# A two-layer attention trunk on one core: first heads' stage length, place of the rotary tables, engine of the accumulators' first step, and order of the output projection

## The chip, the core and the metric

The kernel runs on one core of one Trainium2 chip. The metric is the device time of one execution in microseconds (us). The core's engines work side by side, each through its own queue in order: TensorE (PE: matrix products, with PEld for the loading of the stationary operand), VectorE (DVE), ScalarE (ACT), GpSimd (POOL) and SyncE (SP), which issues most of the DMAs here. They wait for each other on semaphores.

## What is computed

One sequence of 256 positions and 2048 features in float32 passes through two layers. Layer 0 mixes positions by a forgetting attention ("FoX", 16 heads of 128), layer 1 by sliding-window attention; each is followed by a gated feed-forward network with a short convolution. Every sub-layer is modulated by vectors that come from a conditioning vector c:

```python
c_act = jax.nn.silu(c)
for i in range(DEPTH):
    mod = c_act @ ada_w[i] + ada_b[i]
    sh1, sc1, g1, sh2, sc2, g2 = jnp.split(mod[:, None, :], 6, axis=-1)
    h = x * (1.0 + sc1) + sh1
    y = fox_attention(h, ...) if i % 2 == 0 else swa_attention(h, positions, ...)
    x = layer_norm(DEEPNORM_ALPHA * x + (1.0 + g1) * y, ln_mix_g[i], ln_mix_b[i])
    h = x * (1.0 + sc2) + sh2
    y = conv_ffn(h, ...)
    x = layer_norm(DEEPNORM_ALPHA * x + (1.0 + g2) * y, ln_ffn_g[i], ln_ffn_b[i])
```

In FoX a forget gate adds a cumulated bias to the scores:

```python
s = jnp.einsum('bqhd,bkhd->bhqk', qb, kb) * scale + cqb[..., None] - cum[:, :, None, :]
p = jax.nn.softmax(jnp.where(causal, s, -jnp.inf), axis=-1)
o = jnp.einsum('bhqk,bkhd->bqhd', p, v)
return o @ w_o
```

The rotary tables (sine and cosine of the positions) are used in layer 1 alone.

## The kernel before

**Weights.** Every weight matrix streams through in tiles of 256 rows by 512 columns (`stream`). SyncE loads a tile `w` into one of ten buffers, ScalarE casts it to the rounded format of the products (`wh`, L276), VectorE subtracts to get the residual (`wl`, L287), and PE multiplies by both parts, by `wh` first. Each tile is one step of the program; behind it the step calls `run_post` (results that were waiting to be taken over from PSUM), `feed` and `tick`. Casts and residuals each have four buffers, which PE frees. I number the tiles from 0. FoX uses 0 to 127: 0 to 44 in the opening (all of block 0's projections and parts of the other three), 45 to 56 for block 1, 57 to 74 for block 2, 75 to 95 for block 3, and 96 to 127 in the output projection, where two tiles hold four of the sixteen heads for one of four blocks of output columns.

**Heads.** A block makes q, k and v of four heads (0 to 3 in block 0, and so on). `head` and `attend` are generators, which `later(gens, lag)` puts on a list; one of them is started with each tile, and each goes one stage further every `lag` tiles: scores on PE (tile `S`), mask, maximum and softmax (tile `pr`: VectorE L693, exponentials on ScalarE L697, reciprocal on VectorE L703, scaling on ScalarE L705), transposition on PE (`T`, L717) with a copy on ScalarE (`pT`), and the product with v (`o`), which is split into a high and a low half (`oT`, or `hHL` for the last four heads). The heads of a block run beside the tiles of the next. `evac_v` starts them with a lag of 2.

**Background work.** The same list holds `columns` (bias and convolution columns), `rotary` (two DMAs on GpSimd's queue, a cast of the positions, a transposition on PE, some twenty small VectorE instructions, two sines on ScalarE) and `scaled`, which multiplies x by a constant on ScalarE. They are put on it ahead of block 0's step, in the line `later([forget(), columns(), rotary(), scaled()])`.

**Modulation vectors.** The ten vectors of `ada_list` are made beside all this by `ada_vector`: 32 loads `wa` for each, and 32 VectorE instructions of 128x1024 into the single tile `acc`. The first for each half is a product (L404), the others multiply and add (L406); then PE sums over partitions. `ada_tick` spends a rate for each tile, one load and one instruction for each whole unit. After the vector (0, 4) the making is held until the next sub-layer begins, so FoX makes exactly three: (0, 2), (0, 3) and (0, 4).

**Order.** Most instructions may be moved by a scheduler at build time; those under `pin(..., True)` stay in program order on their engine. So the order in which the instructions stand was read from the two built programs.

**Output projection.** `out_proj` takes output blocks 0 and 1 through heads 0 to 7 and 8 to 11, then, as the last heads become ready, through 12 to 15, and then blocks 2 and 3 whole. `residual` takes each block over on VectorE (L621, L622, L624). Behind it `modulate` normalises x (ScalarE L644, VectorE L646), keeps PE awake with idle products (`warm`), and builds the input of the feed-forward network ("the ramp").

Of the kernel before, what the change touches and what calls it, by code (L numbers as in the profile page):

```python
# [21 lines left out]
KC = D // P  # L22
# [19 lines left out]
def hybrid_trunk(ctx: ExitStack, tc: tile.TileContext, a: dict, out: bass.AP):  # L42
    nc = tc.nc
# [28 lines left out]
    def x_banks():  # L72
        return [bank("xs") for _ in range(NT)]
# [136 lines left out]
    def then(fn):  # L210

        work.append(fn)
        if len(work) == 1 and not ahead[0]:
            settle()
# [32 lines left out]
    def defer(gen):  # L247

        post.append(gen)
# [111 lines left out]
    def later(gens, lag=1):  # L361

        bg["wait"].extend((g, lag) for g in gens)
# [23 lines left out]
    cols = {}  # L387
    gates = {}
    ada_list = [(0, 2), (0, 3), (0, 4), (0, 5), (1, 0), (1, 1), (1, 3), (1, 2), (1, 4), (1, 5)]
    ada = {"gen": None, "debt": 0.0, "rate": 0.0, "gate_free": True}  # L390

    def ada_vector(l, v):
        row = v % 3 == 2
        acc = cst.tile([P, D], F32, tag="acc", name="acc")
        part = lambda c, n: acc[:, c:c + n]
        step_ = D // 2
        for k in range(KC):
            for c in range(0, D, D // 2):
                w = wtile("wa").rearrange("p a f -> p (a f)")
                pin(nc.sync.dma_start(w, a["ada_w"][l, k * P:(k + 1) * P, v * D + c:v * D + c + D // 2]), False)  # L400
                for o in range(0, D // 2, step_):
                    ac, wo = part(c + o, step_), w[:, o:o + step_]
                    if k == 0:
                        pin(nc.vector.tensor_scalar_mul(ac, wo, cact[:, 0:1]), True)  # L404
                    else:
                        pin(nc.vector.scalar_tensor_tensor(ac, wo, cact[:, k:k + 1], ac,  # L406
                                                           op0=ALU.mult, op1=ALU.add), True)
                yield
        if row:
            while not ada["gate_free"]:  # L410
                yield
            ada["gate_free"] = False
            g = cst.tile([P, D], F32, tag="gate", name="gate")
            nc.gpsimd.dma_start(g, a["ada_b"][l, v * D:(v + 1) * D].partition_broadcast(P))
            for j in range(D // 512):
                ps = bank()
                mm(ps, ones, acc[:, j * 512:(j + 1) * 512], start=True, stop=True)
                yield
                gj = g[:, j * 512:(j + 1) * 512]
                nc.vector.scalar_tensor_tensor(gj, ps, 1.0, gj, op0=ALU.add, op1=ALU.add)  # L420
            gates[l, v] = g
            return
        ps = bank()
        for k in range(KC):
            pin(mm(ps[:, k:k + 1], part(k * P, P), ones[:, 0:1], start=True, stop=True))
            if k % 4 == 3:
                yield
        cv = cst.tile([P, KC], F32, tag=f"cv{v}", name="cv")
        pin(nc.vector.scalar_tensor_tensor(cv, ps[:, :KC], 1.0 if v % 3 else 0.0,
                                           acol[:, l, v * KC:(v + 1) * KC], op0=ALU.add, op1=ALU.add), True)  # L430
        cols[l, v] = cv
        if v == 4:
            ada["held"] = True
# [15 lines left out]
    def ada_need(l, v):  # L449
        n = 0  # L450
        while (l, v) not in cols and (l, v) not in gates:
            ada_step()
            n += 1
        if n:
            print("caught up", l, v, n)
# [278 lines left out]
    def out_proj(oT, full, w_o, l):  # L734
        def stat(kc, t):
            while kc not in full:
                step()
            return oT[kc][0][:, t * P:(t + 1) * P], oT[kc][1][:, t * P:(t + 1) * P]

        ps = {d: x_banks() for d in range(2)}  # L740

        def part(d, ks):
            use = x_mm_end(ps[d], stat, KC, 2) if d == D // WB - 1 else                 lambda kc, h, l_: x_mm(ps[d], kc, h, l_, stat, KC - 1)
            stream(w_o, 0, d * WB, ks, use)

        for i, ks in enumerate((range(0, 8), range(8, 12))):
            then(lambda i=i: ada.update(rate=((1.4,1.4,1.8,1.8), (0.9,)*4)[l][i]))
            for d in range(2):
                part(d, list(ks))
        then(lambda: ada_need(l, 2))  # L750
        for d in range(D // WB):
            if d < 2:
                part(d, list(range(12, KC)))
            else:
                then(lambda d=d: ada.update(rate=((1.4,1.4,1.8,1.8), (0.9,)*4)[l][d]))
                ps[d] = x_banks()
                part(d, list(range(KC)))
            then(lambda d=d: defer(residual(ps[d], d, gates[l, 2], True)))
        then(lambda: (flush(), ada.update(gate_free=True)))


    def fox(l, j):
# [57 lines left out]
        ready = []  # L820
        oT, full = {}, set()

        def evac_v(ps, V, then, old):
            ps = ps()
            for t in range(NT):
                if old:
                    v = old[t]
                    nc.vector.tensor_tensor(v, ps[t], v, op=ALU.add)
                else:
                    v = f32(gtile("v")).rearrange("p a b -> p (a b)")  # L830
                    nc.scalar.copy(v, ps[t])
                V.append(v)
                yield
            later(then, 2)

        def evac_qk(ps, part, qk, old):
            ps = ps()
# [80 lines left out]
        opening(plan, first_block, {6: forget_load})  # L918
        settle()
        forget_split()  # L920
        later([forget(), columns(), rotary(), scaled()])
        for blk, rate in zip(range(4), (1.0, 1.3, 1.5, 1.6)):
            then(lambda rate=rate: ada.update(rate=rate))
            q, k, V = [], [], []
            n = done.get(blk, 0)

            def more(part, banks_, mul, blk=blk, n=n):
                if n == KC:
                    return lambda: banks[blk, part]
                ps = banks_()  # L930
                stream(w_in, 0, part * FW + blk * WB, list(range(n, KC)), lambda kc, h, l: mul(ps, kc, h, l, n))
                return lambda: ps

            o = [old.get((blk, part)) for part in range(3)]
            wm = lambda ps, kc, h, l, n: w_mm(ps, kc, h, l, first=n)
            pq = more(0, w_banks, wm)
            then(lambda ps=pq, q=q, o=o: defer(evac_qk(ps, 0, q, o[0])))
            pk = more(1, w_banks, wm)
            then(lambda ps=pk, k=k, o=o: defer(evac_qk(ps, 1, k, o[1])))
            pv = more(2, x_banks, lambda ps, kc, h, l, n: x_mm(ps, kc, h, l, hstat, KC - 1, first=n))  # L940
            then(lambda ps=pv, V=V, o=o, hs=[head(blk, hh, q, k, V) for hh in range(4)]: defer(evac_v(ps, V, hs, o[2])))
        out_proj(oT, full, w_o, l)


# [234 lines left out]
```

## Time and profile before

| what | value |
|---|---|
| median of 3 runs (lowest to highest) | 2253.64 us (2253.16 to 2253.78) |
| the profiled execution's own time | 2253.57 us |
| its span, first to last instruction | 2251.8 us |
| opening, to about 127 us | PE busy 105.39 of 127.00 us, DMA at 361 GB/s |
| FoX blocks, 175 to 390 us | VectorE busy 46.26 of 50, 49.82 of 50, 57.91 of 60 and 48.39 of 55 us |
| output projection, 390 to 465 us | PE busy 69.65 of 75 us, VectorE 60.54 |
| ramp, 465 to 495 us | PE busy 28.52 of 30 us |

Rows of stretches (`A:B`) give the length, then busy time and count for PE, PEld, DVE, ACT and POOL, then the granted clock of PE (1.00 is full), the share of the DMA engines and GB/s. Rows in order of time give start and duration in us, engine, line, operation, output and inputs, shape and count; in brackets the idle time of the engine just before, and what ended it. Neighbouring instructions overlap by some 0.07 us on VectorE, so what one costs there is read from start to start. Rows of groups give count, busy time and mean duration in ns, then idle time before them.

### The profile page before, as it was taken

The numbers are of one execution on the slowest core, as the hardware profiler recorded it, in microseconds if no ns is written. First come the engines' busy times: TensorE is split into PE (matmuls) and PEld (weight loads), VectorE is DVE, ScalarE is ACT, GpSimd is POOL, SyncE is SP. The second block draws the span as 40 slices with busy tenths as digits, with TensorE's granted clock in tenths as the row PEclk, the third lists the DMA queues.
The fourth block names the chain that finished last, engine by engine and source line by source line (L and its number), as shares of the span: only waits on it lengthen the run. The fifth ranks groups of instructions, "written<-read, shape, count | busy, mean of one in ns | idle before, by whom it ended". The sixth has DMA issues, their size and how long they took to land.

```text
span 2251.8 us, 33349 instructions
## 1 busy us (share of the span) xinstructions
PE 2201.7 (98%) x12196; PEld 1891.1 (84%) x12196; DVE 1853.0 (82%) x2686; ACT 1193.7 (53%) x1873; POOL 20.0 (1%) x51
## 2 busy tenths in 40 slices
PE   6999999999999999999999999999999999999997
PEld 6988998788888888888887788888888888888886
DVE  7989998889988968978978989889988655666766
ACT  4546644355655433655534578646655533555542
POOL 0000000000000000000000000000000000000000
PEclk9999999999999999999999999999999999999999
DMA  9999999868878889878887867678887556666653
GB/s 351 388 369 312 341 380 352 313 222 311 309 242 275 318 295 329 286 225 285 279 306 266 283 208 256 222 250 292 287 273 244 180 194 195 188 189 192 192 191 117
DMA packets 287429, 602.68 MB, mean 268 GB/s; under 512 B 21846, under 2 KB 55576, under 8 KB 286752
## 3 DMA queue, kind: packets, MB, share of 16 engines
q1 hardware_dynamic: 286208, 595.86, 78.0%
q0 software_dynamic: 1056, 4.69, 0.6%
q8 instruction: 95, 1.56, 0.3%
q14 instruction: 70, 0.57, 0.1%
HBM read 598.37 MB, written 2.10 MB: 267 GB/s over the span
## 4 chain that ended last, share of the span: by engine, by line
PE 82%; DVE 8%; DMA 6%; ACT 2%; issue 2%; SPq 0%; POOL 0%; DVEq 0%; ACTq 0%
PE wd L76 43%; PE xs L76 31%; DMA wo<-in_ada_w_dram 4%; PE ws L76 3%; DVE wl L287 3%; DVE acc L406 2%; PE sm L76 1%; DMA w<-in_fox_w_in_dram 1%; PE o L76 1%; PE S L76 1%; ACT wh L276 1%; DVE pr L693 1%; DMA wa<-in_ada_w_dram 0%; PE warm L76 0%; PE T L717 0%
## 5 line engine op out<-in xcount | busy, mean ns | idle before, releaser
L276 ACT CAST wh<-w 128x1024 fp32r<-128x1024 f32 x728 | 764.6, 1051 | 794.5 <-PE wd L76 300.0
L287 DVE TENSOR_TENSOR wl<-w,wh 128x1024 fp32r<-128x1024 f32 x728 | 887.2, 1221 | 292.7 <-ACT wh L276 277.0
L76 PE MATMUL wd<-hHL,wh 128*128 128x512 f32 x2816 | 717.9, 397 | 1.1 <-DVE hHL L482 1.1
L76 PEld LDWEIGHTS wd<-hHL,wh 128*128 128x128 f32 x2816 | 503.5, 188 | 100.1 <-issue 2.9
L76 PEld LDWEIGHTS wd<-hHL,wl 128*128 128x128 f32 x2816 | 373.3, 188 | 32.8 <-DVE wl L287 1.6
L76 PE MATMUL wd<-hHL,wl 128*128 128x256 f32 x2816 | 379.6, 277 | 1.1 <-DVE wl L287 1.1
L406 DVE SCALAR_TENSOR_TENSOR acc<-wa,cact,acc 128x1024 f32<-128x1024 f32 x300 | 380.3, 1277 | 0.0
L76 PE MATMUL xs<-wh,gT 128*128 128x512 f32 x1408 | 350.0, 390 | 0.0
L76 PEld LDWEIGHTS xs<-wh,gT 128*128 128x128 f32 x1408 | 263.4, 188 | 54.1
L76 PE MATMUL xs<-wl,gT 128*128 128x512 f32 x704 | 189.6, 389 | 0.0
L76 PE MATMUL xs<-wh,hHL 128*128 128x512 f32 x704 | 186.1, 401 | 2.9 <-DVE hHL L86 2.7
L76 PEld LDWEIGHTS xs<-wl,gT 128*128 128x128 f32 x704 | 132.1, 188 | 27.6
L76 PEld LDWEIGHTS xs<-wh,hHL 128*128 128x128 f32 x704 | 129.1, 190 | 29.5 <-DVE hHL L86 3.8
L76 PE MATMUL ws<-hHL,wh 128*128 128x256 f32 x1024 | 133.4, 282 | 9.0 <-ACT wh L276 6.6
L1066 ACT ACTIVATE u<-s,ccol 128x256 f32<-128x256 f32 x176 | 104.7, 600 | 66.4 <-DVE s L1061 48.8
L76 PEld LDWEIGHTS ws<-hHL,wh 128*128 128x128 f32 x1024 | 125.1, 190 | 12.7 <-ACT wh L276 8.5
L76 PE MATMUL xs<-wl,hHL 128*128 128x512 f32 x352 | 98.2, 399 | 1.7 <-DVE wl L287 1.7
L76 PE MATMUL xs<-wh,oT 128*128 128x512 f32 x384 | 98.8, 395 | 0.1
L551 DVE SCALAR_TENSOR_TENSOR oacc<-wo,cact,oacc 128x512 f32<-128x512 f32 x111 | 79.7, 746 | 15.3 <-DMA wo<-in_ada_w_dram 14.8
L1067 DVE SCALAR_TENSOR_TENSOR u<-s,ccol,u 128x255 f32<-128x255 f32 x176 | 84.0, 479 | 5.6 <-ACT u L1066 5.4
L1069 DVE SCALAR_TENSOR_TENSOR u<-s,ccol,u 128x254 f32<-128x254 f32 x176 | 83.8, 477 | 1.1
L76 PEld LDWEIGHTS xs<-wh,oT 128*128 128x128 f32 x384 | 69.9, 188 | 13.9 <-ACT pT L719 0.6
(223 smaller groups left out, 1639.5 us busy)
## 6 DMA issues: line engine op xcount, KB each, us to landing
w<-in_ffn_w_up_dram SPq DMA_DIRECT2D x352, 512.0 KB, 4.6
wa<-in_ada_w_dram SPq DMA_DIRECT2D x320, 512.0 KB, 5.1
w<-in_ffn_w_down_dram SPq DMA_DIRECT2D x176, 512.0 KB, 4.3
w<-in_fox_w_in_dram SPq DMA_DIRECT2D x96, 512.0 KB, 6.6
wo<-in_ada_w_dram SPq DMA_DIRECT2D x128, 256.0 KB, 6.7
w<-in_swa_w_in_dram SPq DMA_DIRECT2D x40, 512.0 KB, 5.4
w<-in_fox_w_o_dram SPq DMA_DIRECT2D x32, 512.0 KB, 5.9
w<-in_swa_w_o_dram SPq DMA_DIRECT2D x32, 512.0 KB, 5.3
```

What stands on the lines that cost most here:

```text
L76: return nc.tensor.matmul(o, lhsT, rhs, start=start, stop=stop, **kw)
L276: pin(nc.scalar.copy(h, w), False)
L287: pin(nc.vector.tensor_tensor(l, w, f32(h), op=ALU.subtract), go in behind)
L406: pin(nc.vector.scalar_tensor_tensor(ac, wo, cact[:, k:k + 1], ac, op0=ALU.mult, op1=ALU.add), True)
L551: nc.vector.scalar_tensor_tensor(ac, wk, cact[:, kc:kc + 1], ac, op0=ALU.mult, op1=ALU.add)
L693: nc.vector.tensor_tensor_reduce(pr[:, b:e].rearrange("p (a k) -> p a k", k=P), S_ps[:, b:e].rearrange("p (a k) -> p a k", k=P), mk, -1.0, ...
L1066: nc.scalar.activation(u, s, AF.Identity, bias=cw(CW, f), scale=cw(2, f))
L1067: nc.vector.scalar_tensor_tensor(u[:, 1:], s[:, :S - 1], cw(1, f), u[:, 1:], op0=ALU.mult, op1=ALU.add)
L1069: nc.vector.scalar_tensor_tensor(u[:, 2:], s[:, :S - 2], cw(0, f), u[:, 2:], op0=ALU.mult, op1=ALU.add)
```

## The change

Four edits. The first instruction of an accumulator goes to ScalarE for the first six vectors of the list. `rotary` and `scaled` are put on the list at block 2 instead of ahead of block 0. The heads of block 0 get a lag of 3 instead of 2. In layer 0's output projection, the first four heads of output block 2 (two tiles) come ahead of the last heads of blocks 0 and 1, and the rate for the rest of block 2 is 1.4 instead of 1.8.

```diff
+    byact = ada_list[:6]
...
-                    if k == 0:
+                    if k == 0 and (l, v) in byact:
+                        nc.scalar.mul(ac, wo, cact[:, 0:1])
+                    elif k == 0:
                         pin(nc.vector.tensor_scalar_mul(ac, wo, cact[:, 0:1]), True)
...
-            then(lambda i=i: ada.update(rate=((1.4,1.4,1.8,1.8), (0.9,)*4)[l][i]))
+            then(lambda i=i: ada.update(rate=((1.4, 1.4), (0.9, 0.9))[l][i]))
             for d in range(2):
                 part(d, list(ks))
+        early = 4 if l == 0 else 0
+        if early:
+            ps[2] = x_banks()
+            part(2, list(range(early)))
         then(lambda: ada_need(l, 2))
...
-                then(lambda d=d: ada.update(rate=((1.4,1.4,1.8,1.8), (0.9,)*4)[l][d]))
-                ps[d] = x_banks()
-                part(d, list(range(KC)))
+                then(lambda d=d: ada.update(rate=((1.4, 1.4, 1.4, 1.8), (0.9,) * 4)[l][d]))
+                n = early if d == 2 else 0
+                ps[d] = ps[d] if n else x_banks()
+                part(d, list(range(n, KC)))
...
-            later(then, 2)
+            later(then, lag)
...
-        later([forget(), columns(), rotary(), scaled()])
+        later([forget(), columns()])
         for blk, rate in zip(range(4), (1.0, 1.3, 1.5, 1.6)):
             then(lambda rate=rate: ada.update(rate=rate))
+            if blk == 2:
+                then(lambda: later([rotary(), scaled()]))
...
-            then(lambda ps=pv, V=V, o=o, hs=[head(blk, hh, q, k, V) for hh in range(4)]: defer(evac_v(ps, V, hs, o[2])))
+            then(lambda ps=pv, V=V, o=o, hs=[head(blk, hh, q, k, V) for hh in range(4)], lag=3 if blk == 0 else 2: defer(evac_v(ps, V, hs, o[2], lag)))
```

The built programs show what this moves. First TensorE at the transpositions of heads 0 to 3. Before, from tile 56 on (`xs` is the sum of a v projection, `ws` of a q or k projection):

```order
L76 MATMUL xs<-wh,hHL 128x512 x3
L717 MATMUL T<-ident,pr 128x128
L76 MATMUL xs<-wh,hHL 128x512
L717 MATMUL T<-ident,pr 128x128 x2
L76 MATMUL xs<-wh,hHL 128x512 x4
L76 MATMUL xs<-wl,hHL 128x512 x4
```

With the change, from the last part of tile 56 to the start of tile 60:

```order
L76 MATMUL xs<-wl,hHL 128x512 x4
L720 MATMUL T<-ident,pr 128x128 x3
L76 MATMUL ws<-hHL,wh 128x256 x16
L76 MATMUL ws<-hHL,wl 128x256 x8
...
L76 MATMUL o<-pT,v 128x256
L76 MATMUL o<-pT,v 128x128
L720 MATMUL T<-ident,pr 128x128 x3
L181 MATMUL sm<-ident,posf 128x2
L76 MATMUL ws<-hHL,wh 128x256 x16
```

Head 0's transposition has moved from inside tile 56 to behind it, the next ones a tile later than before, and the transposition of the positions (`posf`), which stood at tile 48, now follows head 3's.

Second, ScalarE at head 4's softmax, in block 2. Before, between the casts of tiles 67 and 70:

```order
L276 CAST wh<-w 128x1024
L697 ACTIVATE pr,ss<-pr,nm 128x128
L697 ACTIVATE pr,ss<-pr,nm 128x256
L276 CAST wh<-w 128x1024
L845 ACTIVATE qh<-part 128x512
L705 ACTIVATE pr<-pr,ss 128x128
L705 ACTIVATE pr<-pr,ss 128x256
```

With the change, from the cosine table on:

```order
L205 ACTIVATE cost<-nturn 128x16
L276 CAST wh<-w 128x1024 x2
L700 ACT_TABLE_LOAD
L700 ACTIVATE pr,ss<-pr,nm 128x128
L700 ACTIVATE pr,ss<-pr,nm 128x256
L853 ACTIVATE qh<-part 128x512
L708 ACTIVATE pr<-pr,ss 128x128
```

The exponentials now stand behind the sine and cosine tables, one cast more, and a load of the function table.

Third, TensorE in the output projection, at the last heads' products (`o`) and the tiles that need their halves (`hHL`). Before, from tile 107's end on:

```order
L76 MATMUL o<-pT,part 128x128
L717 MATMUL T<-ident,pr 128x128
L76 MATMUL xs<-wh,hHL 128x512
L717 MATMUL T<-ident,pr 128x128 x2
L76 MATMUL xs<-wh,hHL 128x512 x5
L76 MATMUL o<-pT,part 128x256
...
L76 MATMUL xs<-wh,hHL 128x512 x2
L76 MATMUL xs<-wl,hHL 128x512 x4
```

With the change, from the same place:

```order
L76 MATMUL o<-pT,part 128x128
L720 MATMUL T<-ident,pr 128x128 x3
L76 MATMUL xs<-wh,oT 128x512 x8
L76 MATMUL xs<-wl,oT 128x512 x4
L76 MATMUL o<-pT,part 128x256
...
L76 MATMUL xs<-wh,oT 128x512 x8
L76 MATMUL xs<-wl,oT 128x512 x4
...
L76 MATMUL xs<-wh,hHL 128x512 x8
```

Two whole tiles that need only early heads (`oT`) now stand between the products of the last three heads and the first use of their halves.

More of the change, by code (lines that the diff above doesn't have):

```diff
@@ L821, in fox, with evac_v @@
         oT, full = {}, set()
-        def evac_v(ps, V, then, old):
+        def evac_v(ps, V, then, old, lag):
             ps = ps()
```

## The prediction

> **What bounds the kernel now.** I read the page first, then busy time by stretch, then TensorE's order of time wherever it sits idle. The kernel is bound by its matmuls: PE is busy 98% of the span and, in the first feed-forward layer, without a gap.
>
> ```profile
> PE 2201.7 (98%) x12196; PEld 1891.1 (84%) x12196; DVE 1853.0 (82%) x2686; ACT 1193.7 (53%) x1873; POOL 20.0 (1%) x51
> 495.00:880.00 385.00, 385.00 (x2046) 328.64 (x2045) 337.77 (x439) 200.07 (x283) 0.00 (x0) 1.00 0.86 296
> 1250.00:1450.00 200.00, 196.15 (x1015) 161.16 (x1014) 177.17 (x414) 149.99 (x373) 1.36 (x4) 1.00 0.72 241
> ```
>
> So only time that PE loses can be won. In the stretch that the change touches, PE loses it at five places:
>
> ```profile
> 218.68 0.33 PE L717 MATMUL T<-ident,pr 128*128 128x128 f32 x1 [2.41 <-ACT pr L705]
> 402.58 0.73 PE L76 MATMUL xs<-wh,hHL 128*128 128x512 f32 x2 [2.37 <-DVE hHL L86]
> 425.38 1.20 PE L76 MATMUL xs<-wl,oT 128*128 128x512 f32 x4 [1.36 <-DVE wl L287]
> 429.50 1.20 PE L76 MATMUL xs<-wl,oT 128*128 128x512 f32 x4 [1.11 <-DVE wl L287]
> 433.03 1.20 PE L76 MATMUL xs<-wl,oT 128*128 128x512 f32 x4 [0.51 <-DVE wl L287]
> ```
>
> The first is the transposition of head 0's probabilities; the second the output projection waiting for the last heads; the other three wait for weight residuals. After the two longest, the granted clock (last column but two) is halved:
>
> ```profile
> 219.00:220.00 1.00, 1.00 (x5) 0.93 (x4) 1.00 (x6) 0.41 (x3) 0.00 (x0) 0.50 1.07 274
> 221.00:222.00 1.00, 1.00 (x4) 0.81 (x3) 1.00 (x7) 0.39 (x1) 0.00 (x0) 0.50 0.95 373
> 405.00:406.00 1.00, 1.00 (x4) 0.81 (x3) 1.00 (x2) 0.00 (x0) 0.00 (x0) 0.50 0.96 358
> 425.00:426.00 1.00, 0.62 (x3) 0.53 (x4) 1.00 (x3) 0.00 (x0) 0.00 (x0) 1.00 0.94 313
> ```
>
> The same view, microsecond by microsecond, has 3.4 us at half clock after each, so 1.7 us more is lost; the 1.36 us gap left the clock at 1.00. In all 2.41 + 2.37 + 1.36 + 1.11 + 0.51 + 2 x 1.7 = 11.2 us could be won here.
>
> Whether it can depends on VectorE, which is full around the first gap:
>
> ```profile
> 205.00:220.00 15.00, 12.59 (x64) 10.46 (x64) 15.00 (x33) 9.74 (x18) 0.56 (x1) 0.96 0.95 303
> 235.00:250.00 15.00, 15.00 (x131) 14.95 (x130) 15.00 (x17) 6.99 (x10) 0.00 (x0) 1.00 1.00 376
> 250.00:265.00 15.00, 14.65 (x124) 14.21 (x123) 14.93 (x32) 11.72 (x31) 0.00 (x0) 1.00 0.97 336
> ```
>
> **The first accumulators on ScalarE.** An accumulator's first instruction and its neighbours on VectorE:
>
> ```profile
> 177.33 0.74 DVE L404 TENSOR_SCALAR acc<-wa,cact 128x1024 f32<-128x1024 f32 x1
> 177.99 1.22 DVE L287 TENSOR_TENSOR wl<-w,wh 128x1024 fp32r<-128x1024 f32 x1
> 481.72 0.75 DVE L404 TENSOR_SCALAR acc<-wa,cact 128x1024 f32<-128x1024 f32 x1
> 469.60 1.48 ACT L478 ACTIVATE hHL<-sm,B,G 128x256 fp32r<-128x256 f32 x3 [0.48 <-PE sm L508]
> ```
>
> From start to start it holds VectorE 0.66 us. Twelve leave it: six in FoX, two in the ramp behind it, four in the feed-forward layer, where PE has no gap and their 2.6 us are worth nothing. On ScalarE one should take about what the 128x1024 casts take there, 1.04 us (L276, below). The six of FoX fall before 181 us, near 278 and near 354 us, where by the order VectorE is waiting for ScalarE or PE rather than the reverse: worth 0 at the likeliest. In the ramp two leave VectorE (up to 2 x 0.66 = 1.3 us won), but one of the ScalarE products now stands among the normalisations ahead of L478, which had waited only 0.48 us: 1.04 - 0.48 = 0.56 us may be lost. I take the middle, **-0.4 us**.
>
> **The heads and the rotary tables.** The queue of VectorE around head 4:
>
> ```profile
> 188.38 0.42 DVE L806 SCALAR_TENSOR_TENSOR ze<-ze 128x256 f32<-128x256 f32 x1 [0.51 <-ACT ze L804]
> 218.04 0.15 DVE L703 RECIPROCAL ss<-ss 128x2 f32<-128x2 f32 x1
> ...
> 248.73 2.47 DVE L406 SCALAR_TENSOR_TENSOR acc<-wa,cact,acc 128x1024 f32<-128x1024 f32 x2
> ...
> 252.28 1.21 DVE L287 TENSOR_TENSOR wl<-w,wh 128x1024 fp32r<-128x1024 f32 x1
> 253.41 0.15 DVE L703 RECIPROCAL ss<-ss 128x2 f32<-128x2 f32 x1
> ...
> 260.12 0.17 DVE L703 RECIPROCAL ss<-ss 128x2 f32<-128x2 f32 x1
> ...
> 265.47 0.16 DVE L703 RECIPROCAL ss<-ss 128x2 f32<-128x2 f32 x1
> ```
>
> At 188.38 VectorE waits for ScalarE's logarithm, which the change does not move; that is my anchor. Up to head 0's reciprocal the new order has 22 instructions fewer: the rotary ones (some 1.7 us), an accumulation (1.20) and a residual of q (0.6), together 3.4 us. So it stands near 214.7 instead of 218.04, the scores are computed a tile earlier, the transpositions come as one piece behind tile 56, and the wait of 2.41 us and its half clock go.
>
> But the gain does not last. Up to head 7's reciprocal both orders hold the same 135 instructions behind the scan that follows the anchor, 28 accumulations and 19 residuals among them. VectorE has no idle time to give up, so that reciprocal stays at 265.5 us, and by then the rotary work stands in front of heads 4 to 7. Their reciprocals come 1.2 us later for head 4 (an accumulation more ahead), 1.1 for head 5 (a residual more), 2.3 for head 6 (both). PE meanwhile also waits for the position transpose, which now stands right behind head 3's; its operand is cast in VectorE's queue four long instructions after head 3's reciprocal (two accumulations, a residual, a sum of 512 columns: 2.4 + 1.1 + 0.6 = 4.1 us), and tile 60 queues behind it on PE. What PE won is spent there and at heads 4 to 6:
>
> ```profile
> 255.34 0.49 PE L717 MATMUL T<-ident,pr 128*128 128x128 f32 x3
> 262.93 0.49 PE L717 MATMUL T<-ident,pr 128*128 128x128 f32 x3
> 267.60 0.49 PE L717 MATMUL T<-ident,pr 128*128 128x128 f32 x3
> L276 ACT CAST wh<-w 128x1024 fp32r<-128x1024 f32 x22 | 23.0, 1044 | 13.6 <-PE ws L76 8.3 <-DMA w<-in_fox_w_in_dram 3.1 <-PE xs L76 1.1
> L705 ACT ACTIVATE pr<-pr,ss 128x128 f32<-128x128 f32 (+1 forms) x16 | 6.4, 447 | 2.4 <-DVE ss L703 2.4
> L697 ACT ACT_TABLE_LOAD x1 | 1.3, 1283 | 0.0
> ```
>
> Head 6 decides: reciprocal at 260.12 + 2.3 = 262.4; a cast that the new order puts ahead of its scaling ends near 263.4 (it needs the buffer that PE frees at tile 67); half the scaling 0.4: its transposition starts near 263.8, not 262.93. From there to head 7's the work is the same 4.7 us, less one matmul: 268.4 to 268.5 instead of 267.60. I take **+0.9 us**. The low end is head 7's own chain, 265.47 + 0.1 + 0.8 = 266.4: -1.2. The high end lets the second table load (one more than before, 1.28 us, ahead of head 4's exponential) show three quarters of its length: +1.9. From 268 to 396 us PE is full again, with some 0.7 us of waits at heads 10 and 11 in both orders, so this offset is carried on. The two DMAs of the rotary tables keep their place on GpSimd's queue, whose order is the same in both programs, so nothing behind them moves. The scaling of x, which the change moves as well, stands at the same four places of ScalarE's order in both programs: 0.
>
> **The output projection.** Two tiles of the third output block now stand between the last heads' products, so the wait of 2.37 us and its half clock go. The lower rate moves no work out of FoX: three accumulators must be complete by its end, 90 accumulations in both orders. Then VectorE binds:
>
> ```profile
> 396.15 1.23 DVE L287 TENSOR_TENSOR wl<-w,wh 128x1024 fp32r<-128x1024 f32 x1 [0.77 <-ACT wh L276]
> 431.76 1.22 DVE L287 TENSOR_TENSOR wl<-w,wh 128x1024 fp32r<-128x1024 f32 x1
> 443.26 2.00 PE L76 MATMUL xs<-wh,oT 128*128 128x512 f32 x8
> 465.10 2.44 PE L76 MATMUL warm<-ones 128*128 128x512 f32 x10
> ```
>
> Before, the last residual that PE waited for (tile 117) was done at 433.0. In the new order the residual of tile 118 closes this queue: from 396.15 it holds 14 accumulations of 1.20, 11 residuals of 1.13, 12 instructions of 512 columns (0.60) and three of 256 (0.34): 16.8 + 12.4 + 7.2 + 1.0 = 37.4. To this comes about 1.4 us of idle time, since the first output block's sum is asked for (near 407.8) before PE has finished it (near 409.2), and tile 112's residual queues behind that sum. SyncE issues the same loads; those of the two early tiles go ahead of four others, and only ScalarE's casts wait for them, on an engine that the page has at 53%. That gives 435.0. PE then has 0.9 of tile 118, 1.8 of column sums, 2.7 of tile 119 and the 465.10 - 443.26 = 21.8 us of the last eight tiles: 462.3 instead of 465.1, a gain near 2.7 us. But PE arrives at tile 118's residual 2.4 to 2.5 us early, as long a gap as the two that halved the clock; 1.7 us would then go again and 1.0 stay. I take **-1.7 us**, between the two. Low end: without the 1.4 us, and at full clock, -4.0; high end: two half clocks, +0.8.
>
> The Trainium skill, page "TensorE: Matmul & The Clock Gate", section "HAM oscillation — how this bites in real kernels", asks for no idle gap over some 3.4 us; by it this gap leaves the clock alone, and an estimate by that rule is 2251.4 us. The rows above disagree: 2.41 and 2.37 us were enough; by them alone the sum is 2253.1.
>
> In the second layer's attention the scheduler shifts some transpositions by up to two tiles. PE lacks 3.85 of 200 us there; I allow a fifth of it, 0.8, either way, and take 0.
>
> **The sum.** -0.4 + 0.9 - 1.7 = -1.2 us. The profiled execution took 2253.57 us (span 2251.8), 0.07 from the median 2253.64; so 2252.4. The low ends add to -1.3 - 1.2 - 4.0 - 0.8 = -7.3, the high ones to 0.6 + 1.9 + 0.8 + 0.8 = 4.1: 2246.3 to 2257.7.
>
> **The rivals.** *All 11.2 us are won* (2242.4): VectorE does not bind, because its backlog is slack and not need. For it: 4.0 us of accumulator work leave FoX, and residuals are ready early (the one made at 252.28 is tile 67's, and PE starts tile 66 only behind the transposition at 255.34). Against it: the windows at 15.00 of 15, and head 7's probabilities, which are ready at 266.4 for a transposition at 267.60. Chance 0.13.
>
> *The rotary tables strike block 1's heads* (slower): head 4's exponential stands behind sine, cosine, two casts and a table load on ScalarE. If both loads and a cast are exposed, 2 x 1.28 + 1.04 = 3.6 us, and the waits at heads 4 and 5 each halve the clock (3.4), the stage costs 7.0 instead of 0.9: 2258.5. It decides from the point where head 4's transposition starts after 256.2 us, 2.4 us behind PE's arrival near 253.8. For it: the casts wait for DMA and PE in the row of L276; against it: both table loads may run while ScalarE waits anyway. Chance 0.07.
>
> *Nothing changes hands* is the forecast's own middle: the heads' gain is given back, scaling and rate do nothing. The forecast has 0.80, of which 0.10 lies below 2249.1. A measurement here can tell about 0.2%, 4.5 us, from no change: faster 0.13 + 0.10 = 0.23, slower 0.07, same 0.70. The range leaves out the two rivals, 0.20.
>
> **What would show it.** Right: no gap at head 0's transposition, gaps at the position transpose (some 3 us) and at heads 4 to 6 instead; head 7's reciprocal near 265.5; tile 69 near 268.7; no gap behind the last heads, but some four of 1 to 2.5 us at residuals of tiles 113 to 118; warm-up matmuls near 464. Wrong: VectorE idle between 190 and 265 us, head 7 before 266, or the warm-up before 460.

## The result: 0.2% slower

| | before | with the change |
|---|---|---|
| median of 15 runs (lowest to highest) | 2253.64 us (2251.40 to 2254.79) | 2256.77 us (2255.44 to 2262.64) |
| the profiled execution: span | 2251.8 us | 2254.7 us |

The ratio is 1.0019, with a 95% interval of 1.0012 to 1.0026: by the medians the change costs some 3.1 us where 1.2 us of gain were forecast. The time lies inside the stated range, on the other side of no change.

The page of the changed kernel, busy time of each engine, and its windows at the places that the prediction used (columns as in the part on the profile before):

```profile
PE 2199.7 (98%) x12196; PEld 1889.9 (84%) x12196; DVE 1845.3 (82%) x2674; ACT 1207.2 (54%) x1886; POOL 21.6 (1%) x51
205.00:220.00 15.00, 14.60 (x80) 12.26 (x79) 15.00 (x26) 8.40 (x14) 0.57 (x1) 1.00 0.98 330
250.00:265.00 15.00, 12.67 (x107) 12.05 (x106) 15.00 (x32) 11.70 (x26) 0.00 (x0) 1.00 0.95 326
396.00:440.00 44.00, 37.72 (x167) 29.58 (x166) 40.01 (x44) 19.06 (x27) 0.00 (x0) 1.00 0.90 316
```

VectorE is 7.7 us less busy than before (the twelve instructions that left it), ScalarE 13.5 us more; TensorE (PE) has as much to do and waits elsewhere: little between 205 and 220 us, where it stood for 2.4 us, and 2.3 us between 250 and 265 us, where it had stood for 0.35. The waits in PE's order of time (start, length, instruction, and in brackets the idle time ahead of it and what ended it):

```profile
233.32 0.22 PE L181 MATMUL sm<-ident,posf 2*128 2x2 f32 x1 [2.52 <-DVE posf L178]
257.57 0.84 PE L720 MATMUL T<-ident,pr 128*128 128x128 f32 x3 [1.68 <-ACT pr L708]
262.54 0.33 PE L720 MATMUL T<-ident,pr 128*128 128x128 f32 x1 [0.58 <-ACT pr L708]
418.92 0.97 PE L76 MATMUL xs<-wl,hHL 128*128 128x512 f32 x3 [1.56 <-DVE wl L287]
426.57 0.73 PE L76 MATMUL xs<-wl,oT 128*128 128x512 f32 x2 [1.71 <-DVE wl L287]
430.10 0.73 PE L76 MATMUL xs<-wl,oT 128*128 128x512 f32 x2 [0.51 <-DVE wl L287]
438.60 1.19 PE L76 MATMUL xs<-wl,hHL 128*128 128x512 f32 x4 [2.50 <-DVE wl L287]
```

Both old waits, at head 0 and behind the last heads, are gone. One at the transposition of the positions, one each at heads 4 and 5, and four at residuals have taken their place.

**Where the time went, by sections.** Below, each number is the difference to the profile of before in the start of the same weight tile's first product on PE, taken between five tiles: 46, 96, 128, 140 and 720 (before: 182.8, 358.1, 462.3, 503.9 and 2202.2 us). "Half" is the number of 3.41 us stretches at half clock between 215 and 465 us (before has two). The runs e1 to e15 are the experiments below. One run of e7 (3139.92 us) and one of e11 (3142.62 us) were far slower than the rest; they count in the medians, which they move by 0.1 us at most, and not in the ratios.

| kernel | median us | ratio [95%] | up to tile 46 | heads | output projection | ramp | rest | half |
|---|---|---|---|---|---|---|---|---|
| the change | 2256.77 | 1.0019 [1.0012, 1.0026] | +1.6 | +1.3 | -0.1 | +0.4 | -0.3 | 0 |
| e1, the change again | 2259.15 | 1.0030 [1.0016, 1.0044] | -0.1 | +2.0 | +1.3 | +0.3 | -0.2 | 2 |
| e2, heads and rotary | 2255.31 | 1.0008 [0.9999, 1.0017] | +1.0 | +1.4 | 0.0 | 0.0 | -0.4 | 2 |
| e3, accumulators | 2254.18 | 1.0003 [0.9993, 1.0012] | +0.2 | -0.3 | 0.0 | +0.4 | -0.3 | 1 |
| e4, output projection | 2257.39 | 1.0014 [1.0005, 1.0023] | +0.8 | +0.2 | +3.1 | -0.1 | -0.2 | 3 |
| e5, three-tile stage | 2257.13 | 1.0012 [1.0003, 1.0022] | -1.1 | +2.5 | 0.0 | 0.0 | -0.2 | 2 |
| e6, rotary later | 2255.54 | 1.0005 [0.9995, 1.0014] | +0.4 | +2.3 | -0.4 | 0.0 | -0.2 | 2 |
| e7, rotary in the next layer | 2257.52 | 1.0015 [1.0005, 1.0025] | -0.5 | -0.1 | +1.2 | +1.1 | +1.0 | 2 |
| e8, accumulations left out | 2250.28 | 0.9983 [0.9974, 0.9993] | +2.8 | +0.1 | -3.9 | 0.0 | -0.1 | 1 |
| e9, with filling products | 2256.46 | 1.0013 [1.0004, 1.0022] | +0.4 | -0.1 | +6.0 | -0.1 | -0.2 | 4 |
| e10, early tiles, work sooner | 2258.20 | 1.0023 [1.0014, 1.0033] | +1.6 | +6.8 | -2.1 | +1.0 | +0.7 | 3 |
| e11, work sooner | 2259.84 | 1.0026 [1.0015, 1.0037] | +1.1 | +5.9 | -0.3 | -0.1 | -0.3 | 3 |
| e12, early tiles, work later | 2250.68 | 0.9985 [0.9976, 0.9993] | +1.4 | -0.3 | -3.4 | 0.0 | -0.4 | 2 |
| e13, work later | 2249.95 | 0.9984 [0.9975, 0.9993] | -0.4 | -0.3 | -2.4 | 0.0 | -0.2 | 2 |
| e14, the change, work later | 2253.29 | 0.9999 [0.9990, 1.0008] | +0.4 | +1.4 | -3.6 | +1.2 | +0.1 | 2 |
| e15, work later, evenly | 2250.06 | 0.9983 [0.9974, 0.9992] | +0.5 | -0.3 | -3.8 | -0.1 | -0.2 | 1 |

The column up to tile 46 is chance: the same program has +1.6 us in one profile and -0.1 in the other (e1), and runs whose edits all lie behind the opening go from -1.1 to +2.8 us, through waits for DMAs in the opening (113 to 132 us). A profile's span alone would mislead here by half of the difference. Sections that a run's edit does not touch differ by up to 0.4 us as well, and by about 1 us in e7's output projection and e10's ramp.

Without the opening, the first profile of the change is 1.3 us above that of before, with no stretch at half clock, and e1's is 3.4 us above, with two, as many as before has. The 3.1 us between the medians lie between these two. The sections of the first profile had forecasts of -0.4 (ramp), +0.9 (heads) and -1.7 us (output projection) and came out at +0.4, +1.3 and -0.1.

### The profile page after: what moved, and what is told of

Read it like the earlier page. It is cut to its first block, busy times and chain, and to the rows that moved or that the text cites. A ratio compares the mean times of both kernels' runs of the same rounds, so it can differ in the third digit from the quotient of the medians.

```text
span 2254.7 us, 33351 instructions
## 1 busy us (share of the span) xinstructions
PE 2199.7 (98%) x12196; PEld 1889.9 (84%) x12196; DVE 1845.3 (82%) x2674; ACT 1207.2 (54%) x1886; POOL 21.6 (1%) x51
## 4 chain that ended last, share of the span: by engine, by line
PE 73%; issue 12%; DVE 8%; DMA 4%; ACT 3%; SPq 0%; POOL 0%; DVEq 0%; ACTq 0%; POOLq 0%
PE wd L76 43%; PE xs L76 26%; DMA wo<-in_ada_w_dram 3%; DVE wl L287 3%; PE ws L76 2%; DVE acc L409 1%; DMA w<-in_fox_w_in_dram 1%; PE sm L76 1%; ACT wh L276 1%; DVE pr L696 1%; ACT pr L708 0%; DVE oacc L554 0%; DMA w<-in_swa_w_in_dram 0%; PE warm L76 0%; ACT pr L700 0%
## 5 line engine op out<-in xcount | busy, mean ns | idle before, releaser
L76 PEld LDWEIGHTS xs<-wl,hHL 128*128 128x128 f32 x352 | 65.3, 188 | 21.4 <-DVE wl L287 7.7
```

The source lines that it names most:

```text
L76: return nc.tensor.matmul(o, lhsT, rhs, start=start, stop=stop, **kw)
```

## The experiments

### The change again, and its parts

e1 is the changed kernel unaltered. e2 holds the edits of `evac_v` and of the list in `fox`, e3 that of `ada_vector`, e4 that of `out_proj`, each word for word as in the change (shortened here):

```diff
e2:
-        later([forget(), columns(), rotary(), scaled()])
+        later([forget(), columns()])
+            if blk == 2:
+                then(lambda: later([rotary(), scaled()]))
...
-            later(then, 2)
+            later(then, lag)
...
+            then(lambda ps=pv, V=V, o=o, hs=[head(blk, hh, q, k, V) for hh in range(4)], lag=3 if blk == 0 else 2: defer(evac_v(ps, V, hs, o[2], lag)))
e3:
+                    if k == 0 and (l, v) in byact:
+                        nc.scalar.mul(ac, wo, cact[:, 0:1])
e4:
+            part(2, list(range(early)))
...
+                then(lambda d=d: ada.update(rate=((1.4, 1.4, 1.4, 1.8), (0.9,) * 4)[l][d]))
```

> The changed kernel once more. The profile of the changed kernel starts its fox blocks 1.6 us late because of DMA waits in the opening (113 to 132 us), where no edit works. Theory A (chance): another profile has this offset between -1 and +2 us at 140 us, while the differences behind it repeat: about +1.3 us over the heads (140 to 270 us), 0 over the output projection, +0.4 us over the ramp; the time is 1.5 to 3 us above before. Theory B (the change delays the opening): the offset is +1.6 us again and the time is 3 us above before again.

> Only the heads' three-tile stage in block 0 and the rotary tables in block 2. Theory A: the heads' loss stands alone: gap of about 2.5 us at the transposition of the positions, waits at heads 4 and 6, so +1.3 us; no gain at the output projection, since that edit is not in: 2255. Rival (the loss comes from the accumulators, not the heads): within 0.3 us of before, 2253.6.

> Only the first step of six accumulators on ScalarE. Theory A: worth nothing in fox, +0.4 us in the ramp: 2254.0. My prediction's term for it: -0.4 us, 2253.2. Rival (it carries most of the loss, by ScalarE casts that come late in the opening and the first block): +1.5 us or more, 2255.2.

> Only the output projection's order: two tiles of the third block early, and the rates. Theory A: the wait of 2.4 us and its half clock go, stalls of residuals of the same length come: -0.1 us, 2253.5, with the column sums' 3.8 us unmoved in length. My prediction's term: -1.7 us, 2251.9.

The opening's offset did not repeat (-0.1 us), the others did: heads +2.0, ramp +0.3. So theory A on the opening holds; my guess of the time did not, since the median of its six runs came out 5.4 us above before. Where two executions of one program can differ is shown by the output projection: -0.1 us in one profile and +1.3 in the other. (The profiled execution of e1 took 2256.91 us, so the slowest of the six are not explained by it.) The wait of 2.5 us there is the same in both; behind it the clock (last column but two) is not:

```profile
439.00:440.00 1.00, 1.00 (x6) 0.83 (x5) 1.00 (x2) 0.68 (x1) 0.00 (x0) 1.00 0.74 244
```

That is the changed kernel's first profile; the second, a microsecond of the same place:

```profile
438.00:439.00 1.00, 1.00 (x3) 0.76 (x3) 1.00 (x2) 0.67 (x1) 0.00 (x0) 0.50 0.84 277
```

By their sections, e2 and e3 cost what theory A says of heads (+1.4 us) and ramp (+0.4 us); the intervals of both ratios include 1, so the times alone show neither. e4 is the surprise: by itself, the edit that I had counted as the gain carries as much loss as the whole change, and its times spread from 2253.52 to 2260.33 us. In its profile PE waits 2.51 us at the same residual, and then two stretches run at half clock; the column sums of the modulation (`sm<-ones,acc`, products of one column) fall into the first. PE in e4, in order of time:

```profile
436.64 1.21 PE L76 MATMUL xs<-wl,hHL 128*128 128x512 f32 x4 [2.51 <-DVE wl L287]
437.69 0.85 PE L76 MATMUL xs<-wh,hHL 128*128 128x512 f32 x2
438.33 3.41 PE L76 MATMUL sm<-ones,acc 128*128 128x1 f32 x16
441.61 2.91 PE L76 MATMUL xs<-wh,hHL 128*128 128x512 f32 x6
```

Sixteen column sums take 3.41 us here, 1.84 us at full clock in the changed kernel's first profile.

### Heads and rotary tables

e5 has the three-tile stage alone, e6 the later rotary tables alone; e7 has the stage, and the rotary work in neither place but at the start of the feed-forward part (`conv_ffn`):

```diff
e7:
-        later([forget(), columns(), rotary(), scaled()])
+        later([forget(), columns(), scaled()])
...
+            if l == 0 and si == 0:
+                then(lambda: later([rotary()]))
```

> Only the three-tile stage of heads 0 to 3; the rotary work stays in the opening's list. Theory A (VectorE's queue up to head 7 is one sum, 135 instructions; the stage moves work, it removes none): the gap of 2.4 us at head 0 goes, head 7's transposition stays where it was, so 0 to +0.5 us at tile 74 against the start of the fox blocks: 2253.9. Rival (the stage is worth its gap): -2.4 us or better, 2251.

> Only the rotary tables in block 2, heads 0 to 3 as before. Theory A (it is the rotary work, put in front of heads 4 to 7 with two table loads of ScalarE and the transposition of the positions on TensorE, that costs the heads their time): +1 to +2 us at tile 74 against the start of the fox blocks, 2255.0. Rival (the stage of three tiles costs it): within 0.5 us of before.

> The three-tile stage, and the rotary tables neither ahead of heads 0 to 3 nor ahead of heads 4 to 7 but in the first feed-forward layer, where TensorE has no gap and VectorE has idle time. Theory A: VectorE has some 22 instructions (1.7 us) fewer up to head 7, ScalarE two table loads and four casts fewer; the gap at head 0 goes and no other comes: -1.5 to -3 us at tile 74, 2251.5. Rival (VectorE fills the place with accumulations, so nothing is won): 0, 2253.7.

e5 went against both theories: the gap at head 0 is gone, but one of 2.80 us stands at head 2, with a half clock, and 2.5 us are lost. e6 loses 2.3 us, a little more than theory A says, with 1.75 us of waiting at the positions, and 2.19 us and a half clock at head 4. In these profiles each half alone costs more than both together, so neither "is" the loss; by the medians that holds for e5 (3.3 us above before, e2 1.6), while e6 (1.8) can't be told from e2. The wait in e5 and the one in e6:

```profile
232.81 0.84 PE L717 MATMUL T<-ident,pr 128*128 128x128 f32 x3 [2.80 <-ACT pr L705]
```
```profile
233.92 0.19 PE L181 MATMUL sm<-ident,posf 2*128 2x2 f32 x1 [1.75 <-DVE posf L178]
```

e7 shows what limits these heads. Without any rotary work VectorE reaches head 7's reciprocal 1.75 us sooner after the scan than before, as theory A says, yet PE comes to tile 96 no sooner (-0.1 us): head 6's reciprocal stands 1.7 us later in that order, and from head 6's transposition to head 7's PE itself is full. What is cleared away for one head is spent on another. That e7's median is 3.7 us above before all the same comes from behind the heads: two half clocks in the output projection, +1.1 us in the ramp and +1.0 in the rest. I did not follow these up.

### What binds the output projection

e8 leaves out eight accumulations of one modulation vector; e9 fills PE's wait with products by zeros:

```diff
e8 (with e4):
-                    else:
+                    elif (l, v) != (0, 4) or k < 12:
                         pin(nc.vector.scalar_tensor_tensor(ac, wo,
e9 (with e4, in x_mm ahead of the residual's products):
+        for n in range(fill):
+            mm(ps[ts[0]], zr.bitcast(F32R), h[:, n % 2, :])
```

> The output projection's new order alone (as in the run of that edit), and the last eight accumulations of the scale vector of layer 0's feed-forward modulation are left out, so the output is not the reference's; their loads stay. Theory A (the accumulations on VectorE keep the residuals late, so the new order only moves the stall): 8 x 1.2 = 9.6 us leave VectorE ahead of the last residual, the four stalls (1.8 + 1.8 + 0.6 + 2.7 us) and the half clock behind the last go: 6 to 7 us faster than the new order without half clock, 2247. Rival (TensorE's order, loads or casts bind there): within 2 us of before.

> The output projection's new order alone, with eight more products of 128x512 by a block of zeros (about 2 us of TensorE, adding nothing) put ahead of the residual's products at the wait of 2.5 us. Theory C (the clock is judged in stretches of 3.41 us whose phase differs between executions; a stretch with 1.86 us or more of idle time is followed by one at half clock, and none with 1.73 us or less was): the wait shrinks to some 0.6 us, the half clocks behind it go, the end of the wait stays where VectorE's residual sets it: 2254 to 2254.5, and the times spread over 3 us rather than 7. Rival (the half clocks have another cause, or the eight products cost their own 2 us): 2257 or more, as the new order without them (2257.4, 2253.5 to 2260.3).

e8 gains 3.9 us in the projection where 6 to 7 were expected: the wait of 2.5 us and that of 0.6 are gone, but the first two stay:

```profile
419.02 1.19 PE L76 MATMUL xs<-wl,hHL 128*128 128x512 f32 x4 [1.60 <-DVE wl L287]
426.67 1.19 PE L76 MATMUL xs<-wl,oT 128*128 128x512 f32 x4 [1.67 <-DVE wl L287]
```

Ahead of the first nothing was left out. Ahead of the second, two accumulations are missing (in e4 they start at 419.75 us and take 2.4 us), but the scheduler put four other instructions of 0.6 us in their place (L624, L622, L621 and L624, from 423.01 us in e8), so the residual comes no sooner. So VectorE's queue does bind there. e9 says nothing on the clock: eight column sums that wait for an accumulation had slipped between the filling products and the residual's, PE waited 1.96 us for them behind the filling, and three stretches in a row ran at half clock. A wait filled where it no longer was. PE in e9:

```profile
437.30 1.35 PE L76 MATMUL sm<-ones,acc 128*128 128x1 f32 x8 [1.96 <-DVE acc L410]
```

Then the place of the accumulations. e10 and e11 do more of them in the blocks, e12 and e13 fewer ahead of the residuals and the rest in the fourth output block; e15 paces e13 more evenly; e14 is the whole change with e12's pace:

```diff
e10 (with e4), e11 (alone):
-        for blk, rate in zip(range(4), (1.0, 1.3, 1.5, 1.6)):
+        for blk, rate in zip(range(4), (1.0, 1.3, 1.7, 1.8)):
e12 (with e4), e13 (alone), e14 (with the whole change):
+            then(lambda i=i: ada.update(rate=((1.4, 1.0), (0.9, 0.9))[l][i]))
...
+                then(lambda d=d: ada.update(rate=((1.4, 1.4, 1.0, 2.0), (0.9,) * 4)[l][d]))
e15 (alone):
+            then(lambda i=i: ada.update(rate=((1.4, 1.2), (0.9, 0.9))[l][i]))
...
+                then(lambda d=d: ada.update(rate=((1.4, 1.4, 1.2, 1.2), (0.9,) * 4)[l][d]))
```

> The output projection's new order alone, with the rates of the modulation work raised in the third and fourth block (1.7 and 1.8 for 1.5 and 1.6), so that 87 instead of 80 of its VectorE instructions stand ahead of the projection's thirteenth tile. Theory A (VectorE's queue binds at the residuals): the four stalls (1.8 + 1.8 + 0.6 + 2.7 us) lose most of their length, up to 8.4 us of VectorE time is gone from there, and some comes back as waits at heads 8 to 15 in the blocks: -2 to -6 us against before, 2250. Rival (VectorE has no room in the blocks either): the heads of the last two blocks lose as much, 2254 to 2257.

> The kernel before, with only the raised rates of the third and fourth block. Theory A: the three stalls of residuals (1.5 + 1.3 + 0.7 us) go, the wait for the last heads (2.4 us and its half clock in most executions) stays: -2 to -3.5 us, 2251. Rival (no room in the blocks): 2253.5 to 2256.

> The output projection's new order alone, but with the modulation work paced down in it (1.4 for its first eight tiles, 1.0 up to the third output block, 2.0 in the fourth) so that 88 instead of 94 of its VectorE instructions stand ahead of the residual of the third block's fifth tile (tile 118), and the rest where VectorE has 9.7 us of idle time (442 to 466 us). Theory A (what keeps the residuals late is accumulations that nothing needs before the ramp): the four stalls (1.8 + 1.8 + 0.6 + 2.7 us) and the half clocks behind the last go and nothing comes for them: 6 to 8 us faster than before, 2247. Rival (the sums are needed by then, the ramp waits for them): the same time is lost at 465 to 475 us, 2252 to 2254.

> The kernel before with that pace alone, no early tiles. Theory A: its three stalls (1.5 + 1.3 + 0.7 us) go, the wait for the last heads (2.4 us, with 1.7 us for a half clock behind it in most executions) stays: 3 to 3.5 us faster, 2250.3; so the early tiles are worth the rest, 3 to 4 us. Rival (the early tiles are worth nothing even with room on VectorE): the same as the early tiles with that pace, within 1 us.

> The whole change, with the slower pace of the modulation work in the output projection (as in the run e12). Theory A (the parts add up: the output projection's loss is mended by the pace, heads and rotary tables keep their +1.5 to +2.2 us, the first steps on ScalarE their +0.4): 1.7 to 2.5 us above e12 (2250.7), so 2252.4 to 2253.2. Rival (the later heads of this kernel leave VectorE another queue there, so the pace does not help it): 2255 or more.

> The kernel before with the pace 1.2 from its ninth tile of the output projection to its end (e13: 1.0, then 2.0), so that the last accumulations end a tile earlier and the column sums spread over three tiles. Theory A (what e13 gives back at 441 us is TensorE at column sums that wait for the last accumulation, and half clocks in stretches filled by one-column products): the wait of 1.5 us shrinks below 0.8 us and the half clocks behind it go or halve, 2247.5 to 2249. Rival (the wait only moves, 91 instead of 89 accumulations ahead of tile 118's residual bring its stalls back): 2250 or more.

Sooner is worse: in e11 the waits at residuals shrink, and 5.9 us are lost in the blocks ahead of tile 96 (6.8 in e10); the rivals hold, and both times lie above even what they allowed. Later is better, by 3.2 us with the early tiles (e12, where 6 to 8 were forecast) and 3.9 us without them (e13). Both are faster than before, and the rival of e13 holds as well: once VectorE has room, the early tiles are worth nothing that these runs can tell. The output projection in windows, first e4, then e13:

```profile
396.00:440.00 44.00, 37.74 (x165) 29.66 (x163) 41.53 (x44) 17.46 (x23) 0.00 (x0) 0.98 0.88 309
440.00:466.00 26.00, 26.00 (x118) 21.87 (x118) 13.39 (x19) 7.38 (x7) 0.00 (x0) 0.91 0.68 235
```
```profile
396.00:440.00 44.00, 43.55 (x195) 35.38 (x193) 42.68 (x47) 17.83 (x20) 0.00 (x0) 1.00 0.91 317
440.00:466.00 26.00, 24.60 (x112) 20.68 (x112) 15.46 (x26) 9.73 (x12) 1.73 (x3) 0.87 0.61 218
```

PE is busy 43.55 of the first 44 us instead of 37.74; even the wait behind the last heads, which the change had removed by other means, is gone. The order on VectorE suggests why: before, it splits the last heads' products into halves (L86) three in a row from 402.11 us, behind two accumulations; in e13 the splits stand one by one between the accumulations, the last at 401.56 us. So e13 met its forecast time (2250.3 us) by luck: theory A had let this wait stay. Not all of the gain is kept. PE and its clock in e13 at the end of the third output block:

```profile
441.40 2.70 PE L76 MATMUL sm<-ones,acc 128*128 128x1 f32 x16 [1.47 <-DVE acc L406]
443.96 3.76 PE L76 MATMUL xs<-wh,oT 128*128 128x512 f32 x8
446.00:447.00 1.00, 1.00 (x4) 0.81 (x3) 1.00 (x2) 0.00 (x0) 0.00 (x0) 0.50 0.70 227
```

The column sums now wait 1.47 us for the last accumulation, and two stretches at half clock follow; in e12 they wait 1.75 us, and one follows. e15 fits the reading and brings no gain: with the sums a tile earlier that wait and those half clocks are gone from its profile, while waits at residuals are back (0.51, 1.11 and 0.52 us), and the time is e13's. e14 nearly adds up as theory A says: 2.6 us above e12 where 1.7 to 2.5 were expected, from heads (+1.7 against e12) and ramp (+1.2, three times what the first steps on ScalarE explain; I did not find the rest).

## Why the prediction was wrong, step by step

**The first accumulators: -0.4 was forecast, +0.4 came.** In FoX they are worth nothing, as said (VectorE waits longer at the same places). In the ramp the high end was right: one product stands among the normalisations and takes 1.14 us, not the 1.04 of a cast. ScalarE in the changed kernel:

```profile
470.40 0.80 ACT L647 ACTIVATE x<-x,rs 128x512 f32<-128x512 f32 x1
471.11 1.14 ACT L405 ACTIVATE acc<-wa,cact 128x1024 f32<-128x1024 f32 x1
472.15 0.80 ACT L647 ACTIVATE x<-x,rs 128x512 f32<-128x512 f32 x1
472.86 1.45 ACT L481 ACTIVATE hHL<-sm,B,G 128x256 fp32r<-128x256 f32 x3
```

PE's wait for the feed-forward input that is built behind it (`hHL`) grew from 0.53 us before to 0.98:

```profile
474.58 0.70 PE L76 MATMUL wd<-hHL,wh 128*128 128x512 f32 x2 [0.98 <-DVE hHL L485]
```

No gain from the two instructions that left VectorE shows in the ramp of the three profiles with this edit and no other pace (+0.4, +0.3 and +0.4 us in the change, e1 and e3); taking the middle between the bounds was the mistake.

**Heads and rotary tables: +0.9 forecast, +1.3 to +2.0 came.** The mechanism was right, the size too small. VectorE's anchor and head 7's reciprocal in the changed kernel, and ScalarE's scaling behind it:

```profile
189.98 0.42 DVE L814 SCALAR_TENSOR_TENSOR ze<-ze 128x256 f32<-128x256 f32 x1 [0.51 <-ACT ze L812]
228.76 0.17 DVE L706 RECIPROCAL ss<-ss 128x2 f32<-128x2 f32 x1 [0.89 <-ACT pr L700]
267.64 0.14 DVE L706 RECIPROCAL ss<-ss 128x2 f32<-128x2 f32 x1
268.27 1.06 ACT L276 CAST wh<-w 128x1024 fp32r<-128x1024 f32 x1 [0.78 <-PE ws L76]
269.23 0.80 ACT L708 ACTIVATE pr<-pr,ss 128x128 f32<-128x128 f32 x2
```

From the anchor to head 7's reciprocal it is 77.66 us, against 265.47 - 188.38 = 77.09 before: the sum of 135 instructions held, plus some 0.6 us; the wait of 0.89 us for ScalarE at head 3 is new. Two things were not priced: that wait, and that the gap at the positions (2.52 us where "some 3 us" was written) can halve the clock. It did so in e1, e2 and e14 and not in the first profile. And head 6 did not decide alone: PE stood still for 2.52 us at the positions, 1.68 at head 4 and 0.58 at head 5, and came to head 6's transposition without a wait. The claim that from head 6's transposition to head 7's the work is the same held too: 270.53 - 265.63 = 4.9 us, for 4.7; the cast that now stands ahead of head 7's scaling makes it late by over a microsecond, but PE was not there before.

**The output projection: -1.7 forecast, -0.1 to +3.1 came.** This step failed. The residual of tile 118 came at 438.6 us, 437.0 without the opening's 1.6 us and 435.7 without the heads' 1.3, for 435.0 forecast: nearly right. Behind it I counted 1.8 us of column sums; three rows of before, where they stand ahead of the last eight tiles (from 443.26 us), and three of the changed kernel show what there is:

```profile
434.32 1.92 PE L76 MATMUL sm<-ones,acc 128*128 128x1 f32 x16
438.49 0.95 PE L76 MATMUL sm<-ones,acc 128*128 128x1 f32 x8
439.62 0.95 PE L76 MATMUL sm<-ones,acc 128*128 128x1 f32 x8
```
```profile
440.09 1.84 PE L76 MATMUL sm<-ones,acc 128*128 128x1 f32 x16
444.19 0.95 PE L76 MATMUL sm<-ones,acc 128*128 128x1 f32 x8
447.85 0.95 PE L76 MATMUL sm<-ones,acc 128*128 128x1 f32 x8
```

They are 32, 3.7 us in the changed kernel: 1.9 more than in the sum. With these and the 0.7 us of the residual, the gain of 2.7 us at full clock is 0.1, which is what the first profile shows. The half clock, of which I counted a part as certain, comes by chance: no stretch of it followed this wait in the first profile, one in e1 and two in e4.

**And the step that mattered was never taken.** "The lower rate moves no work out of FoX", since 90 accumulations must be done by its end, is right. From that I went on as if their place within FoX were fixed too. Before, VectorE had 10.5 us of idle time between 440 and 466 us (15.48 of 26 busy), behind the last residual that PE waits for:

```profile
440.00:466.00 26.00, 26.00 (x118) 21.55 (x118) 15.48 (x24) 9.61 (x10) 0.56 (x1) 1.00 0.62 214
```

The rival that all 11.2 us are won was refused because VectorE's windows were full; six accumulations moved a few tiles later (e12, e13) show that for the projection's part the fullness was an order and no need.

**Signs that were named:** no gap at head 0, one at the positions, waits at heads 4 and 5 (none at 6), head 7's reciprocal at 266.0 without the opening's offset (265.5), tile 69 at 269.2 (268.7), four waits of 0.5 to 2.5 us at tiles 113 to 118, the warm-up products at 466.3 (464; tile 69 and these also without that offset). The profile is much as forecast; the sum was not.

## What to carry to other kernels

Where background work shares an engine with the work that another engine waits for, look for idle time of that engine **behind** the last wait before adding cover ahead of it: here six accumulations placed later won 3 to 4 us, while two tiles brought forward won nothing. Count every small instruction between the last wait and the end of the stage from the rows, not from one group of them. And a wait may cost more than its length by the clock, in some executions and not in others: compare two profiles of one program before a difference of 2 us is explained.

## What the runs showed of the hardware

**The clock is judged in stretches of 3.41 us on a grid.** Within one execution all half-clock stretches begin whole multiples of 3.413 us apart (before: 126.71, 218.87 and 403.19 us are 27 and 54 stretches apart), and the grid lies differently in each execution. The Trainium skill, page "TensorE: Matmul & The Clock Gate", section "What's actually happening", has this window, 3413 ns and free-running; the traces agree. It also asks for a whole idle window before the clock drops; here much less was enough. I laid the grid over the 17 profiles of before, the change and the experiments and added, stretch by stretch, PE's idle time and the time in one-column products (from start to start). From the first record of the clock (at some 20 us) to 2236 us, of 42 stretches at full clock that a half-clock one followed, all had 1.86 us or more; of some 10,900 others, two had more than 1.78 (1.92 both). So a wait of 2.4 to 2.5 us halves the clock or not, by how it falls on the grid: of the 23 waits of 2.37 to 2.59 us between 205 and 465 us, 17 were followed by half clock. Waits up to 1.7 us were not, unless column sums fell into the same stretch. Examples are the 2.52 us at the positions, which the grid cut into 1.36 and 1.15 us in the changed kernel's first profile, and the 3.04 us in e1, which lay in one stretch:

```profile
234.00:235.00 1.00, 1.00 (x11) 1.00 (x11) 1.00 (x2) 1.00 (x4) 0.00 (x0) 1.00 1.08 356
```
```profile
234.00:235.00 1.00, 1.00 (x7) 1.00 (x6) 1.00 (x2) 0.30 (x1) 0.00 (x0) 0.50 0.96 377
```

**Column sums seem to count as idle time for the clock.** In e10 a stretch without any gap, but with 2.02 us of one-column products, was followed by half clock. Eight of the 42 stretches had less than 1.5 us without work on PE (0 to 1.49), and reach 2.0 to 3.3 us only with their column sums. In e4 and e13 the column sums took 3.0 and 1.6 us of a stretch at half clock, and a second followed (6.83 us in one piece). In e9 even a third followed (10.24 us), behind a stretch with only 0.7 us of them, which this does not explain. All this rests on coincidences in many profiles; the run that was to test the clock by filling a wait (e9) did not, so that filling restores the clock is not shown.
